# The halves of the weight chunks at moving places, and loads five chunks ahead, in a two-layer decoder

## The chip, the cores and the metric

The kernel runs on one core of one Trainium2 chip. The metric is the device time of one execution, in microseconds (us), taken as the median of several runs. The engines are named as in the profile: PE (TensorE matmuls), PEld (its weight loads), DVE (VectorE), ACT (ScalarE), POOL (GpSimd) and SP (SyncE, which here issues nearly all DMAs; SPq is its queue).

## The reference: a decoder trunk of two layers

All is float32: 256 tokens, width 2048, feed-forward width 5632.

- Layer 0: h += gMLP(rmsnorm(h)): z = gelu(x W_in), split into u and v; v is normed and mixed over tokens by a causal 128 x 128 matrix per group; (u * mixed) W_out. Then h += convFFN(rmsnorm(h)): x W_up, a causal convolution of width 3 per channel, silu(gate) * value, W_down.
- Between the layers, shared keys, values and forget gates: rmsnorm(h) W_kvf, keys normed per head.
- Layer 1: forgetting attention (16 heads of 128, with its own queries and output gate), then the same kind of convFFN with its own weights.
- A last rmsnorm.

The weights are some 418 MB, each used once, for 256 tokens.

## The kernel before

**Float32 by two halves.** Every operand of the large products is the sum of two fp32r values: hi (a rounded copy) and lo (the rest). A product a*b is computed as hi*hi + hi*lo + lo*hi. Activations are kept as one tile with both parts beside each other, `[128, K/128, 512]`: columns 0 to 255 hi, 256 to 511 lo, for one 128-row of features each. Such tiles are X1 (the normed residual, in the profile X), `mlp_X2`, `att_X2` and H (`ffn0_H`, `ffn1_H`; in the profile ffn_H).

**The weight stream.** The weights come in 786 chunks of 128 x 1024 float32 (512 KB; two half chunks at the very start, and one smaller for the forget gates). The class `Stream` holds them in one list, in the order of use. For each chunk there are three steps:

- `_load` (L62 to L71): SP issues the DMA into a `raw` tile. The tile has `LOADS - AHEAD + 1` buffers, which is 4.
- `_split` (L73 to L84): ACT copies raw into `whi` (L82), DVE writes raw - hi into `wlo` (L83). Both tiles have `AHEAD + 1`, 4, buffers of 4096 bytes a partition.
- `mult`: the matmuls of the chunk.

`run` (L86 to L102) goes through the list: in step i it issues the load of chunk i + 6 (`LOADS`), the split of chunk i + 3 (`AHEAD`), and the matmuls of chunk i. After them `advance` moves every pending generator one step: these are the epilogues (evictions, convolution, norms, attention heads), so their instructions come between the chunks in each engine's order. The order of each engine is the order of the program; a buffer is written again when its last readers are done. So the load of a chunk waits in SP's queue for the DVE half of the split of the chunk that had its raw buffer.

**Two kinds of chunk.** All matmuls are recorded at one helper line (L165).

- A feature chunk (`feat_block`, L167): 4 rows of 128 features by 256 outputs. The weights are stationary, 128 x 128 at a time, and the activations move. hi takes eight matmuls of 512 columns (both parts of the activation), lo takes eight of 256 columns (the hi part alone). A pair of outputs (m = 0, 1) alternates between two PSUM banks. In the last chunk of a block lo comes first. There are 656 such chunks: 416 move X1 (W_in's u half, both W_up, the output gate), 176 move H (both W_down), 32 move `mlp_X2` and 32 `att_X2`.
- A token chunk (`tok_block`, L190): 2 rows of 128 features by 512 outputs. The activations are stationary, and the weights move, 512 columns at a time: for each of two token halves hi by hi, lo by hi, hi by lo. There are 129, two of them halves, for W_in's v half, the queries, the keys and the values.

**Where things lie.** Tiles lie in SBUF in the order in which they are made in a pool, each rounded up to 32 bytes: col, h, X1, acc, rB, rcol, ident, ones; then the stream's pool (4 raw, 4 whi, 4 wlo); then small tiles (warm, sq, rsqrt's scratch, half); then the pool of the phase (mlp, ffn0, att, ffn1), which begins with X2 or H.

**The start.** The input x comes in eight slices (`load_input`), each loaded in front of a chunk of the first token block, and prepared (`input_prep`, into X1) in front of that chunk's split. Two tiles for the token mixing of 1 MB each (`load_mix`, L348) are loaded by SP in front of the first chunk of the third token block.

Of the kernel before, what the change touches and what calls it, by code (L numbers as in the profile page):

```python
# [11 lines left out]
F32R = mybir.dt.float32r  # L12
# [5 lines left out]
P = 128  # L18
# [4 lines left out]
KF = FFN // P  # L23
NH = 16
CHUNK = 1024
EPS = 1e-6
SCALE = 128 ** -0.5
AHEAD = 3
LOADS = 6
NEG = -3e38  # L30


# [7 lines left out]
class Stream:  # L40
# [21 lines left out]
    def _load(self, i):  # L62
# [3 lines left out]
        if src is None:  # L66
            return
        raw = self.pool.tile([P, CHUNK], F32, name="raw", tag="raw", bufs=LOADS - AHEAD + 1)
        raw = raw[:, :src.shape[1]]
# [3 lines left out]
    def _split(self, i):  # L73
        if self.items[i][3]:
            self.items[i][3]()
        raw = self.raw.pop(i, None)
        if raw is None:
            return
        n = raw.shape[1]
        hi = self.pool.tile([P, CHUNK], F32R, name="whi", tag="whi")  # L80
        lo = self.pool.tile([P, CHUNK], F32R, name="wlo", tag="wlo")
        self.nc.scalar.activation(hi[:, :n], raw, AF.Copy)  # L82
        self.nc.vector.tensor_tensor(lo[:, :n], raw, hi[:, :n].bitcast(F32), op=OP.subtract)  # L83
        self.parts[i] = (hi, lo)  # L84

    def run(self):  # L86
        n = len(self.items)
        for i in range(-LOADS, n):
            if 0 <= i + LOADS < n:
                self._load(i + LOADS)  # L90
            if 0 <= i + AHEAD < n:
# [41 lines left out]
def build(ctx, tc, d, out):  # L133
# [94 lines left out]
    def rsqrt(y, v, n):  # L228

        t = small.tile([P, n], F32, name="rs_t", tag=f"rs_t{n}", bufs=2)  # L230
        nc.vector.tensor_scalar(y.bitcast(I32), v.bitcast(I32), -0.5, 1597463007.0, op0=OP.mult, op1=OP.add)
        for _ in range(3):
            nc.vector.scalar_tensor_tensor(t, y, -0.5, y, op0=OP.mult, op1=OP.mult)
            nc.vector.tensor_tensor(t, t, v, op=OP.mult)
            nc.vector.scalar_tensor_tensor(y, t, 1.5, y, op0=OP.add, op1=OP.mult)

    def token_sums(rest=None):
# [7 lines left out]
        v = small.tile([P, 2], F32, name="ts_v", tag="ts_v", bufs=2)  # L245
        nc.vector.tensor_scalar(v, mp[:, :2], 1.0 / D, EPS, op0=OP.mult, op1=OP.add)
        rsqrt(rcol, v, 2)
# [108 lines left out]
    def v_done(blk):  # L356
        def done(ps):
# [8 lines left out]
            if blk == 3:  # L366
                v = small.tile([P, 2], F32, name="ts_v", tag="ts_v", bufs=2)
                rv = ph.keep("rv", [P, 2])
                nc.vector.tensor_reduce(v, ss, axis=AX.X, op=OP.add)
                nc.vector.tensor_scalar(v, v, 1.0 / D, EPS, op0=OP.mult, op1=OP.add)  # L370
                rsqrt(rv, v, 2)
# [78 lines left out]
    def head_norm(key, blk, gain):  # L450

        def done(ps):
            dst = att(key)
            for tb in range(2):
# [5 lines left out]
                nc.vector.tensor_reduce(v, sq.rearrange("p (a b) -> p a b", a=4), axis=AX.X, op=OP.add)  # L460
                nc.vector.tensor_scalar(v, v, 1.0 / P, EPS, op0=OP.mult, op1=OP.add)
                rsqrt(r, v, 4)
# [192 lines left out]
def feat_chunks(w, order=None):  # L655
# [5 lines left out]
    a = a.reshape(K // 512, 4, P, N // 256, 256)  # L661
    return np.ascontiguousarray(a.transpose(3, 0, 2, 1, 4)).reshape(-1, P, CHUNK)


def tok_chunks(w):

    K, N = w.shape
    a = w.reshape(K // 256, 2, P, N // 512, 512)
    return np.ascontiguousarray(a.transpose(3, 0, 2, 1, 4)).reshape(-1, P, CHUNK)

# [42 lines left out]
```

## Time and profile before

| | |
|---|---|
| median of 3 runs | 2261.58 us (2261.07 to 2261.91) |
| the profiled execution: its time, its span | 2261.96 us, 2260.2 us |
| mean granted TensorE clock | 0.997 |
| PE busy | 2239.9 us, 99%, 12440 matmuls |
| PEld busy | 1930.5 us, 85% |
| DVE busy | 1529.2 us, 68% |
| ACT busy | 1191.5 us, 53% |
| read from HBM | 417.88 MB, mean 186 GB/s over the span |

The span runs from the first to the last instruction of one execution. Busy times add up the instructions of an engine; those of PE overlap one another, so a busy PE says that matmuls are under way, not how fast they follow one another. How fast is read from the starts of instructions in order of time, or from the number of matmuls in a window.

### The profile page before, as it was taken

The page shows a single profiled execution, that of the slowest core. Times are in us where ns is not written, and L with a number is a line of the kernel's source. Part 1 is how long each engine was busy: PE and PEld are TensorE (multiplying, and loading weights), DVE is VectorE, ACT ScalarE, POOL GpSimd, SP SyncE. Part 2 cuts the span into 40 slices and gives each one's busy share as a digit, 9 for nine tenths or more (in the row PEclk, how much of TensorE's full clock was granted, in tenths as well). Part 3 has the DMA queues.
Part 4 walks back from the last instruction along what each step waited for, and adds up shares of the span by engine and source line. Part 5 has one row for each costly group of instructions (what it writes and reads, how often), then busy time and mean ns, then how long its engine had stood idle before and what let it go on. Part 6 is the DMA issues. An engine that isn't in the chain of part 4 may idle for free.

```text
span 2260.2 us, 32221 instructions
## 1 busy us (share of the span) xinstructions
PE 2239.9 (99%) x12440; PEld 1930.5 (85%) x12440; DVE 1529.2 (68%) x2212; ACT 1191.5 (53%) x1622; POOL 34.6 (2%) x56
## 2 busy tenths in 40 slices
PE   8999999999999999999999999999999999999997
PEld 6888888888888888888788888888888888888886
DVE  6576677777777755457786567677777777764554
ACT  6544455555555544345444666446555555553442
POOL 3000000000000000000000110000000000000000
PEclk9999999999999999999999999999999999999998
DMA  7555555555555555555565555555556555556553
GB/s 280 187 191 170 187 192 190 192 190 193 188 187 187 196 186 176 201 187 171 170 189 183 164 164 187 178 194 187 190 193 190 193 188 194 187 179 202 188 186 113
DMA packets 116442, 422.11 MB, mean 187 GB/s; under 512 B 13232, under 2 KB 13376, under 8 KB 116032
## 3 DMA queue, kind: packets, MB, share of 16 engines
q1 hardware_dynamic: 115344, 417.93, 56.2%
q0 software_dynamic: 768, 2.10, 0.4%
q8 instruction: 97, 1.59, 0.3%
q14 instruction: 57, 0.47, 0.1%
q10 hardware_dynamic: 176, 0.02, 0.0%
HBM read 417.88 MB, written 2.11 MB: 186 GB/s over the span
## 4 chain that ended last, share of the span: by engine, by line
PE 98%; DVE 1%; ACT 0%; DMA 0%; issue 0%; SPq 0%; DVEq 0%
PE ps L165 96%; PE mp L387 0%; PE mp L471 0%; PE mp L557 0%; PE mp L572 0%; DMA h<-xT 0%; DVE wlo L83 0%; DVE X L221 0%; PE mp L580 0%; PE mp L581 0%; PE mp L556 0%; PE mp L579 0%; DVE h L313 0%; PE mp L243 0%; ACT X L220 0%
## 5 line engine op out<-in xcount | busy, mean ns | idle before, releaser
L83 DVE TENSOR_TENSOR wlo<-raw,whi 128x1024 fp32r<-128x1024 f32 (+1 forms) x786 | 953.6, 1222 | 391.2 <-ACT whi L82 383.6
L82 ACT ACTIVATE whi<-raw 128x1024 fp32r<-128x1024 f32 (+1 forms) x786 | 822.5, 1053 | 390.4 <-PE ps L165 355.6
L165 PE MATMUL ps<-X,whi 128*128 128x512 f32 x3328 | 829.6, 396 | 0.0
L165 PEld LDWEIGHTS ps<-X,whi 128*128 128x128 f32 x3328 | 602.3, 188 | 120.7
L165 PEld LDWEIGHTS ps<-X,wlo 128*128 128x128 f32 x3328 | 425.9, 188 | 28.3
L165 PE MATMUL ps<-X,wlo 128*128 128x256 f32 x3328 | 430.6, 277 | 0.0
L165 PE MATMUL ps<-ffn_H,whi 128*128 128x512 f32 x1408 | 354.2, 395 | 0.0
L165 PEld LDWEIGHTS ps<-ffn_H,whi 128*128 128x128 f32 x1408 | 253.5, 188 | 48.3
L165 PEld LDWEIGHTS ps<-ffn_H,wlo 128*128 128x128 f32 x1408 | 190.4, 188 | 14.6
L275 ACT ACTIVATE half<-ps 128x512 f32<-128x512 f32 x104 | 62.1, 597 | 256.0 <-PE ps L165 256.0
L165 PE MATMUL ps<-ffn_H,wlo 128*128 128x256 f32 x1408 | 193.3, 281 | 0.0
L276 DVE TENSOR_TENSOR ffn_a<-ps,half 128x512 f32<-128x512 f32 x88 | 60.9, 692 | 175.3 <-ACT half L275 175.3
L165 PE MATMUL ps<-whi,X 128*128 128x512 f32 x512 | 163.6, 397 | 6.3 <-ACT whi L82 6.3
L165 PE MATMUL ps<-whi,att_X 128*128 128x512 f32 x512 | 169.3, 402 | 0.0
L421 DVE SCALAR_TENSOR_TENSOR ffn_c<-ffn_a,col,ffn_c 128x255 f32<-128x255 f32 x352 | 161.7, 480 | 6.3
L417 ACT ACTIVATE ffn_c<-ffn_a,col 128x256 f32<-128x256 f32 x176 | 96.4, 595 | 47.1 <-DVE ffn_a L277 47.1
L165 PEld LDWEIGHTS ps<-whi,X 128*128 128x128 f32 x512 | 97.1, 190 | 27.2 <-ACT whi L82 6.3
L165 PEld LDWEIGHTS ps<-whi,att_X 128*128 128x128 f32 x512 | 96.1, 188 | 22.2
L165 PE MATMUL ps<-wlo,X 128*128 128x512 f32 x256 | 101.0, 395 | 1.1 <-DVE wlo L83 1.1
L165 PE MATMUL ps<-wlo,att_X 128*128 128x512 f32 x256 | 101.0, 395 | 0.0
L220 ACT ACTIVATE X<-h,col 128x256 fp32r<-128x256 f32 x64 | 29.0, 501 | 104.1 <-DVE h L284 101.5
L225 ACT ACTIVATE ffn_H<-ffn_c 128x256 fp32r<-128x256 f32 x88 | 36.9, 419 | 69.5 <-DVE ffn_c L425 69.5
(140 smaller groups left out, 1228.8 us busy)
## 6 DMA issues: line engine op xcount, KB each, us to landing
raw<-up SPq DMA_DIRECT2D x352, 512.0 KB, 3.7
raw<-down SPq DMA_DIRECT2D x176, 512.0 KB, 4.2
raw<-a_in_u SPq DMA_DIRECT2D x32, 512.0 KB, 3.6
raw<-a_out SPq DMA_DIRECT2D x32, 512.0 KB, 4.1
raw<-b_q SPq DMA_DIRECT2D x32, 512.0 KB, 4.3
raw<-kvf_k SPq DMA_DIRECT2D x32, 512.0 KB, 4.0
raw<-kvf_v SPq DMA_DIRECT2D x32, 512.0 KB, 3.7
raw<-b_g SPq DMA_DIRECT2D x32, 512.0 KB, 3.3
```

The source lines that it names most:

```text
L82: self.nc.scalar.activation(hi[:, :n], raw, AF.Copy)
L83: self.nc.vector.tensor_tensor(lo[:, :n], raw, hi[:, :n].bitcast(F32), op=OP.subtract)
L165: nc.tensor.matmul(o, a, b, start=start, stop=stop, skip_group_check=True)
L220: nc.scalar.activation(dst[:, kt, :T], h[:, kt, :], AF.Copy, scale=g)
L225: nc.scalar.activation(dst[..., :T], src, AF.Copy)
L275: nc.scalar.activation(t, ps[:, :, T:], AF.Copy)
L276: nc.vector.tensor_tensor(a, ps[:, :, :T], t, op=OP.add)
L417: nc.scalar.activation(c[:, m, :], a[:, m, :], AF.Identity, scale=w[2], bias=column(C_CONVB + l * 2 * KF + f))
L421: nc.vector.scalar_tensor_tensor(c[:, m, n:], a[:, m, :T - n], w[k], c[:, m, n:], op0=OP.mult, op1=OP.add)
```

## The change

Each `whi` and `wlo` buffer becomes 128 elements (512 bytes) longer. The part that is used, still 1024 elements, begins at an offset that goes with the number i of the list item: 16 x (i mod 32) bytes for hi, 16 x (7i mod 32) for lo. Since 7 and 32 have no common factor, both go through 32 places in 32 chunks, in different orders. `LOADS` goes from 6 to 5, by which `raw` has three buffers in place of four, and the load of chunk i + 5 is issued in step i. Splits stay three chunks ahead.

```diff
 CHUNK = 1024
+PAD = 128
 ...
 AHEAD = 3
-LOADS = 6
+LOADS = 5
 ...
         n = raw.shape[1]
-        hi = self.pool.tile([P, CHUNK], F32R, name="whi", tag="whi")
-        lo = self.pool.tile([P, CHUNK], F32R, name="wlo", tag="wlo")
+        hi = self.pool.tile([P, CHUNK + PAD], F32R, name="whi", tag="whi")
+        lo = self.pool.tile([P, CHUNK + PAD], F32R, name="wlo", tag="wlo")
+        hi = hi[:, 4 * (i % 32):][:, :CHUNK]
+        lo = lo[:, 4 * (7 * i % 32):][:, :CHUNK]
         self.nc.scalar.activation(hi[:, :n], raw, AF.Copy)
```

In bytes per partition: raw 4 x 4096 becomes 3 x 4096, whi and wlo 8 x 4096 become 8 x 4608; the sum is the same.

## The prediction

> **What bounds the kernel now.** I read the page first: span, engine shares, the chain that ended last.
>
> ```profile
> span 2260.2 us, 32221 instructions
> PE 2239.9 (99%) x12440; PEld 1930.5 (85%) x12440; DVE 1529.2 (68%) x2212; ACT 1191.5 (53%) x1622; POOL 34.6 (2%) x56
> ```
>
> ```profile
> PE 98%; DVE 1%; ACT 0%; DMA 0%; issue 0%; SPq 0%; DVEq 0%
> ```
>
> TensorE (PE) holds 98% of the chain, so I asked next what it waits for, and what the queue that loads the weights waits for. Columns of the waits: total us, times, longest.
>
> ```profile
> PE ps L165 <- DVE wlo L83: 1.1, 3, 0.4
> ```
>
> ```profile
> SPq L70 <- DVE wlo L83: 1534.0, 587, 8.9
> ```
>
> Once started, the matmuls of the weight stream wait 1.1 us in all for their weights. A saturated PE can still be slow, so the third view is the windows, which give matmuls per 100 us (the count behind PE), and the fourth the order of time, where the start of a run of matmuls less the start of the run before gives the real interval (the mean ns of one overlaps its neighbours).
>
> ```profile
> 600.00:700.00 100.00, 100.00 (x579) 87.06 (x578) 76.11 (x110) 59.18 (x83) 0.00 (x0) 1.00 0.59 190
> 800.00:900.00 100.00, 100.00 (x570) 87.21 (x568) 52.42 (x54) 40.06 (x45) 0.00 (x0) 1.00 0.56 187
> ```
>
> ```profile
> 599.41 2.02 PE L165 MATMUL ps<-X,whi 128*128 128x512 f32 x8
> 601.27 1.07 PE L165 MATMUL ps<-X,wlo 128*128 128x256 f32 x8
> 602.19 2.02 PE L165 MATMUL ps<-X,whi 128*128 128x512 f32 x8
> ```
>
> ```profile
> 806.92 1.11 PE L165 MATMUL ps<-ffn_H,wlo 128*128 128x256 f32 x8
> 807.87 2.02 PE L165 MATMUL ps<-ffn_H,whi 128*128 128x512 f32 x8
> 809.74 1.11 PE L165 MATMUL ps<-ffn_H,wlo 128*128 128x256 f32 x8
> ```
>
> Both windows have the clock at 1.00 and PE at 100%, yet X gives 579 matmuls and ffn_H 570 for the same mix of sizes. The runs say where: the eight 512-column matmuls with hi take 1.86 us on X (599.41 to 601.27) and 1.87 on ffn_H; the eight 256-column ones with lo take 0.92 us on X (601.27 to 602.19) but 0.95 on ffn_H (806.92 to 807.87), 119 ns each against 115. A chunk is 2.78 us on X (599.41 to 602.19; 16 x 100/579 = 2.76) and 2.82 on ffn_H (806.92 to 809.74; 16 x 100/570 = 2.81).
>
> These are the same instructions on the same weight buffers, and what differs is where the moving tile lies. By the sizes of the tiles in the order in which they are made, each rounded up to 32 bytes, whi and wlo lie 64 bytes past X1 within 512 (rcol and ones are the only odd sizes between), and 288 past H (224 bytes of small tiles follow wlo). The three tiles that are H, the mlp X2 and the att X2 begin at one address. So the trace already holds two of the 32 relative places: **64, at 2.77 us a chunk, and 288, at 2.81** (means of the two readings).
>
> **The change part by part.** *Instructions:* none is added or removed; splits stay at 786 and matmuls at 12440. The split's operands move by multiples of 16 bytes, its lengths don't:
>
> ```profile
> L83 DVE TENSOR_TENSOR wlo<-raw,whi 128x1024 fp32r<-128x1024 f32 (+1 forms) x786 | 953.6, 1222 | 391.2 <-ACT whi L82 383.6
> L82 ACT ACTIVATE whi<-raw 128x1024 fp32r<-128x1024 f32 (+1 forms) x786 | 822.5, 1053 | 390.4 <-PE ps L165 355.6
> ```
>
> I cost the shifted split at nothing. The cover is PE's lead: whi waited for PE for 355.6 us, so the split stands ready before it is wanted. Were each split a tenth longer, 0.12 us x 786 = 96 us would fall on a DVE that is 68% busy, behind PE. Only a split so long that DVE fills up would show.
>
> *Addresses:* one raw buffer less frees 4 KB, and 8 x 512 bytes take 4 KB, so every other tile stays where it is, and every buffer of hi and lo still begins at the same place within 512. Place p of hi is p = i mod 32, of lo 7i mod 32. Both kinds of chunk then walk through all 32 relative places (X from 64, ffn_H from 288), so both should come to the same mean, if the relative place is what counts.
>
> *What the mean of the places is* is the price that decides. Rows for the counts:
>
> ```profile
> L165 PE MATMUL ps<-X,whi 128*128 128x512 f32 x3328 | 829.6, 396 | 0.0
> L165 PE MATMUL ps<-ffn_H,whi 128*128 128x512 f32 x1408 | 354.2, 395 | 0.0
> ...
> L165 PE MATMUL ps<-mlp_X,whi 128*128 128x512 f32 x256 | 63.8, 396 | 0.0
> L165 PE MATMUL ps<-att_X,whi 128*128 128x512 f32 x256 | 63.7, 395 | 0.0
> ```
>
> That is 3328/8 = 416 chunks on X and (1408 + 256 + 256)/8 = 240 on the other address. Of the 32 places I know two, 2.77 and 2.81; their mean is 2.79. X loses 0.02 us x 416 = 8.3 us and the others gain 0.02 x 240 = 4.8: **+3.5 us**. The bounds: if the mean is as good as X's place, 240 x -0.04 = -9.6; if it is as bad as ffn_H's, 416 x 0.04 = +16.6. A third sample is the forget chunk, where the weights are only 16 columns and walk by 64 bytes per pair against one moving address:
>
> ```profile
> 1113.01 0.40 PE L165 MATMUL ps<-att_X,whi 128*16 128x512 f32 x1
> ...
> 1117.86 0.40 PE L165 MATMUL ps<-att_X,whi 128*16 128x512 f32 x1
> ```
>
> Fourteen pairs in 4.85 us are 0.346 a pair, 2.77 for eight: X's value, by loads an eighth as long. It pulls towards the lower bound, but those loads have less to collide with, so I stay with the middle. All places seen so far are multiples of 32 bytes; half of the new ones aren't, and no row prices those.
>
> The token chunks stream the weights and hold X. Their rows, one hi pair per three matmuls:
>
> ```profile
> 59.85 0.62 PE L165 MATMUL ps<-whi,X 128*128 128x512 f32 x2
> ...
> 69.47 0.62 PE L165 MATMUL ps<-whi,X 128*128 128x512 f32 x2
> ...
> 1137.86 0.40 PE L165 MATMUL ps<-wlo,att_X 128*128 128x512 f32 x1
> 1138.56 0.39 PE L165 MATMUL ps<-wlo,att_X 128*128 128x512 f32 x1
> ```
>
> 14 threes in 9.62 us are 229 ns a matmul on X, and 0.70 us a three are 233 on att_X. With 768 matmuls each, a mean of 231 costs 1.5 us on the one and gives 1.5 on the other: **0**, bounds -3 and +3.
>
> *Loads five ahead.* A load waits until the split of the chunk that had its buffer is done (the 1534 us of SP's waits above): now the chunk four before it, then three, so each load goes out about one chunk later. All that SP issues in this order moves with it (the input slices, the second part of col, the two mixing tiles). A steady case:
>
> ```profile
> 606.59 0.33 SPq L70 DMA_DIRECT2D raw<-up  x1
> 609.89 1.22 DVE L83 TENSOR_TENSOR wlo<-raw,whi 128x1024 fp32r<-128x1024 f32 x1
> 615.34 1.06 ACT L82 ACTIVATE whi<-raw 128x1024 fp32r<-128x1024 f32 x1 [0.48 <-PE ps L165]
> ```
>
> ```profile
> DMA to landing us min/median/max: 2.8/3.9/9.7
> ```
>
> The load at 606.59 is split at 615.34. Afterwards it goes out at 611.1 (609.89 + 1.22) and lands at 615.0 by the median: still before ACT wants it. It may be some tenths late by a slower landing, and PE has three split chunks, 8.3 us, in hand. Price 0 there; without that lead half a microsecond per block of four chunks would be about 100 us. Two places have less in hand. They are the start and the loading of the mixing tiles:
>
> ```profile
> 27.04 1.06 ACT L82 ACTIVATE whi<-raw 128x1024 fp32r<-128x1024 f32 x1 [2.24 <-DMA raw<-a_in_v]
> ...
> 39.49 0.42 SPq L351 DMA_DIRECT2D mlp_bB<-bs  x1
> ...
> 50.43 1.06 ACT L82 ACTIVATE whi<-raw 128x1024 fp32r<-128x1024 f32 x1 [4.88 <-DMA raw<-a_in_v]
> ...
> 55.48 0.69 ACT L361 ACTIVATE mlp_vt<-ps,rcol 128x512 f32<-128x512 f32 x1 [2.70 <-PE ps L165]
> ```
>
> At the start ACT already waits 2.24 us for a chunk, at 27.04, and PE hardly sees it: its waits there, the 1.1 us above, are for DVE's lo. Loads one chunk later, 2.8 us, prolong such waits of ACT. Behind the mixing tiles the split at 50.43 opens the next block, which PE begins when it ends the one evicted at 55.48. 2.8 us later it ends at 54.3, and its lo at 55.5: just in time. Both places together 0 to 4 us; I take **+0.5**, near the end that the rows favour.
>
> *Sum:* 3.5 + 0 + 0.5 = +4.0 us. The profiled execution took 2261.96 us, 1.76 more than its span, and lies 0.4 above the median of 2261.58; the change in the span carries over: 2261.6 + 4.0 = **2265.6**.
>
> **The rivals.** *The place does nothing (no effect beyond the loads).* The intervals could differ by the moving tile's own place, 32 bytes past a multiple of 64 for X and at one for H, and not by the distance to the weights. Then shifting the weights moves nothing, and the time is 2261.6 to 2262.6. For it: hi takes the same 1.86 and 1.87 us at both distances. Against it: the token chunks, whose moving tile is the weights, also differ, 229 to 233. The Trainium skill is on this rival's side: "TensorE: Matmul & The Clock Gate", in its step-by-step part, says that moving rows and weight loads have two independent read ports, so that loading the next weights takes nothing from the running matmul; by that rule the answer would be 2261.6. The trace does not settle it.
>
> *The mean place is like ffn_H's (slower).* X's lo at 115 ns is the shortest interval of a 256-column matmul in these rows. If X sits at one of few free places, 416 chunks lose it: +16.6 us, nothing for the others, 2278.7; with places worse than both, 2.84 say, 0.07 x 416 + 0.03 x 240 = +36, 2298. It decides from a mean of 2.792 on: 656 chunks x (2.792 - 2.785, the weighted mean now) is 4.5 us. For it: the 115; against it: the forget chunk at 2.77.
>
> *A fixed distance is the disease (faster).* 512 columns take 229 ns in the token chunks on X, and 233 everywhere else. If most places give 229 and 115, a chunk is 8 x 344 = 2.75: -0.02 x 416 - 0.06 x 240 = -23 us, 2239; half of that is 2250. Against it: hi is alike at both known distances.
>
> **How the numbers follow.** A measurement of this kernel tells about 0.2%, 4.5 us, from no change. The forecast (mean between the two places) has 0.42, its own range 2252 to 2274; no place effect 0.13; like ffn_H or worse 0.22; faster 0.23. The forecast lies close to the edge: of its 0.42, 0.20 is slower, 0.19 within, 0.03 faster. With 0.01 of the rival without effect: slower 0.43, same 0.31, faster 0.26. The range reaches half into both outer rivals, to 2240 and 2284, leaving out some 0.12 below and 0.08 above.
>
> **What would show it.** Right: the 100-us windows on X fall from 579 to about 575 matmuls and those on ffn_H rise from 570 to about 575; chunk lengths repeat every 32 chunks; the intervals of lo on X spread from 115 upwards. Wrong: windows unchanged (no place effect), both below 570 (bad places), both above 579 (cured). The loads are right if matmuls of the weight stream wait for whi or wlo no more than 1 us beyond now; ACT waiting for raw a few us more is expected and costs nothing. Any wait of PE for wlo in the windows after 100 us makes the load step wrong.

## The result, and the profile after

The changed kernel takes **2275.52 us** (median of 4; 2273.80 to 2275.98), the kernel before 2261.74 (median of 4) measured beside it. The ratio is **1.0060, interval 1.0047 to 1.0073**: 13.8 us, or 0.6%, slower. That is three times the 0.2% that can be told from no change. It lies inside the predicted range, 1.5 us outside the forecast's own range, and 9.9 us above the predicted time.

The page of the changed kernel, its span and engines, then its chain that ended last:

```profile
span 2273.9 us, 32221 instructions
PE 2250.8 (99%) x12440; PEld 1942.4 (85%) x12440; DVE 1530.0 (67%) x2212; ACT 1191.9 (52%) x1622; POOL 35.0 (2%) x56
...
PE 97%; DVE 2%; DMA 1%; ACT 0%; issue 0%; POOL 0%; SPq 0%; DVEq 0%; ACTq 0%; POOLq 0%
```

The instructions are the same in number, 32221, and PE still holds nearly the whole chain. The span grew by 13.7 us (2260.2 to 2273.9) and PE's busy time by 10.9, so most of the loss lies where PE is at work. (Three lines were added: L165 of before is L168 here, L82 and L83 are L85 and L86, L471 is L474.)

Groups by line and form, busy us, mean ns of one, idle us. The two rows of before that the prediction did not show:

```profile
L165 PE MATMUL ps<-X,wlo 128*128 128x256 f32 x3328 | 430.6, 277 | 0.0
...
L165 PE MATMUL ps<-ffn_H,wlo 128*128 128x256 f32 x1408 | 193.3, 281 | 0.0
```

and the four groups of the changed kernel:

```profile
L168 PE MATMUL ps<-X,whi 128*128 128x512 f32 x3328 | 827.1, 395 | 0.0
L168 PE MATMUL ps<-X,wlo 128*128 128x256 f32 x3328 | 444.8, 281 | 0.0
L168 PE MATMUL ps<-ffn_H,whi 128*128 128x512 f32 x1408 | 352.8, 394 | 0.0
L168 PE MATMUL ps<-ffn_H,wlo 128*128 128x256 f32 x1408 | 192.1, 280 | 0.0
```

One group lost: lo on X, 430.6 to 444.8, **+14.2 us**. The other three gained: hi on X 829.6 to 827.1 (-2.5), hi on ffn_H 354.2 to 352.8 (-1.4), lo on ffn_H 193.3 to 192.1 (-1.2).

The windows of the changed kernel (number of matmuls is the count behind PE):

```profile
400.00:500.00 100.00, 100.00 (x574) 87.38 (x573) 76.03 (x108) 58.99 (x81) 0.00 (x0) 1.00 0.58 187
600.00:700.00 100.00, 100.00 (x570) 87.17 (x569) 75.36 (x108) 58.69 (x81) 0.00 (x0) 1.00 0.57 187
800.00:900.00 100.00, 100.00 (x575) 87.54 (x574) 52.12 (x53) 41.55 (x45) 0.00 (x0) 1.00 0.58 188
```

On X 579 has become 570 to 574, on ffn_H 570 has become 575, with the clock at 1.00 and PE at 100% in all of them. In order of time:

```profile
640.13 1.08 PE L168 MATMUL ps<-X,wlo 128*128 128x256 f32 x8
641.05 2.02 PE L168 MATMUL ps<-X,whi 128*128 128x512 f32 x8
642.90 2.04 PE L168 MATMUL ps<-X,wlo 128*128 128x256 f32 x16
644.78 1.57 PE L168 MATMUL ps<-X,whi 128*128 128x512 f32 x6
```

The first eight lo take 0.92 us (640.13 to 641.05), 115 ns each; the next sixteen, of two other chunks, 1.88 (642.90 to 644.78), 117.5 each. So lo now differs from chunk to chunk. To see how, I took, for every matmul of the feature chunks, the time from its start to the start of the next matmul, sorted by the place of the half against the moving tile. Places are bytes, and only their remainder by 256 is kept, since places 256 apart came out alike (within about 1 ns; an experiment below tries it at one place). Mean ns, 208 matmuls each:

| place past X1 | 0 | 16 | 32 | 48 | 64 | 80 | 96 | 112 |
|---|---|---|---|---|---|---|---|---|
| lo, 256 columns | 118.3 | 118.6 | 117.8 | 119.8 | **115.6** | 119.2 | 117.8 | 119.6 |
| hi, 512 columns | 233.1 | 231.3 | 233.9 | 233.0 | 235.8 | 232.1 | 234.8 | 233.4 |

| place past X1 | 128 | 144 | 160 | 176 | 192 | 208 | 224 | 240 |
|---|---|---|---|---|---|---|---|---|
| lo, 256 columns | 119.5 | 120.1 | 119.5 | 118.3 | 116.4 | 116.8 | 117.3 | 118.4 |
| hi, 512 columns | 234.2 | 232.6 | 234.1 | 230.7 | 233.3 | 231.9 | 233.4 | 229.4 |

Of sixteen places the one that the kernel before held on X all the time, 64, is the best for lo, and the worst for hi. The table has to be read with care: both offsets go by the same i, so each place of lo always meets the same place of hi (lo at 64 meets hi at 64, lo at 16 meets hi at 240), and what it prices are sixteen pairs, each also behind the same chunk. Means over all: lo on X 114.0 before and 118.3 now, hi on X 233.7 and 232.9; on the other address (H and the two X2, where the place was 32) lo 118.8 and 118.0, hi 232.8 and 231.9. The lengths of neighbouring X chunks repeat every 16 chunks (over the 176 chunks of the first W_up the correlation is 0.87 at a distance of 16 chunks, and -0.05 at 15).

As sums: X, 3328 x (118.3 - 114.0) = +14.3 and 3328 x (232.9 - 233.7) = -2.4 us; the other address, 1936 matmuls of either kind, -1.5 and -1.7. Together **+8.7 us by places**. The remaining 5.0 of the span's 13.7 lie in token chunks and in epilogues between them. PE's waits in the changed kernel that bear on it (total us, times, longest):

```profile
PE mp L474 <- DVE att_big L468: 2.5, 2, 2.4
PE mp L246 <- POOL acc L273: 1.5, 1, 1.5
```

Neither of them is a wait for weights, and neither is among PE's waits in the kernel before. The experiments take the two parts in turn.

### The profile page after: what moved, and what is told of

Read it like the earlier page. It is cut to its first block, busy times and chain, and to the rows that moved or that the text cites. A ratio compares the mean times of both kernels' runs of the same rounds, so it can differ in the third digit from the quotient of the medians.

```text
span 2273.9 us, 32221 instructions
## 1 busy us (share of the span) xinstructions
PE 2250.8 (99%) x12440; PEld 1942.4 (85%) x12440; DVE 1530.0 (67%) x2212; ACT 1191.9 (52%) x1622; POOL 35.0 (2%) x56
## 4 chain that ended last, share of the span: by engine, by line
PE 97%; DVE 2%; DMA 1%; ACT 0%; issue 0%; POOL 0%; SPq 0%; DVEq 0%; ACTq 0%; POOLq 0%
PE ps L168 95%; DVE wlo L86 0%; PE mp L390 0%; PE mp L474 0%; PE mp L560 0%; DMA raw<-a_in_v 0%; DMA h<-xT 0%; PE mp L575 0%; DMA raw<-kvf_k 0%; ACT whi L85 0%; PE mp L583 0%; PE mp L584 0%; PE mp L559 0%; PE mp L582 0%; DVE h L316 0%
## 5 line engine op out<-in xcount | busy, mean ns | idle before, releaser
L86 DVE TENSOR_TENSOR wlo<-raw,whi 128x1024 fp32r<-128x1024 f32 (+1 forms) x786 | 953.4, 1221 | 413.3 <-ACT whi L85 405.2
L85 ACT ACTIVATE whi<-raw 128x1024 fp32r<-128x1024 f32 (+1 forms) x786 | 822.5, 1053 | 420.1 <-PE ps L168 302.4
L168 PE MATMUL ps<-X,whi 128*128 128x512 f32 x3328 | 827.1, 395 | 0.0
L168 PEld LDWEIGHTS ps<-X,whi 128*128 128x128 f32 x3328 | 603.7, 188 | 119.8
L168 PEld LDWEIGHTS ps<-X,wlo 128*128 128x128 f32 x3328 | 437.0, 188 | 27.4
L168 PE MATMUL ps<-X,wlo 128*128 128x256 f32 x3328 | 444.8, 281 | 0.0
L168 PE MATMUL ps<-ffn_H,whi 128*128 128x512 f32 x1408 | 352.8, 394 | 0.0
L168 PEld LDWEIGHTS ps<-ffn_H,whi 128*128 128x128 f32 x1408 | 253.4, 188 | 48.0
L168 PEld LDWEIGHTS ps<-ffn_H,wlo 128*128 128x128 f32 x1408 | 188.5, 188 | 14.0
L168 PE MATMUL ps<-ffn_H,wlo 128*128 128x256 f32 x1408 | 192.1, 280 | 0.0
L168 PE MATMUL ps<-whi,X 128*128 128x512 f32 x512 | 164.2, 398 | 6.2 <-ACT whi L85 6.2
L168 PE MATMUL ps<-whi,att_X 128*128 128x512 f32 x512 | 169.7, 403 | 0.0
L168 PEld LDWEIGHTS ps<-whi,X 128*128 128x128 f32 x512 | 97.0, 189 | 28.1 <-ACT whi L85 6.2
L168 PEld LDWEIGHTS ps<-whi,att_X 128*128 128x128 f32 x512 | 96.9, 189 | 21.7
L168 PE MATMUL ps<-wlo,X 128*128 128x512 f32 x256 | 102.2, 399 | 0.0
L168 PE MATMUL ps<-wlo,att_X 128*128 128x512 f32 x256 | 101.3, 396 | 0.0
```

The lines of the kernel that those rows point to most:

```text
L168: nc.tensor.matmul(o, a, b, start=start, stop=stop, skip_group_check=True)
```

## The experiments

Except where said, the diff is against the kernel before, and the ratio is to the kernel before beside it. Interval means are worked out as above, from all starts of a kind.

**The loads alone.**

```diff
-LOADS = 6
+LOADS = 5
```

> The kernel before with LOADS = 5 alone; the weights keep their places. Theory (most of the 13.8 us is the places, the loads cost little): +1 to +4 us against before, from a later start (0.8 us by 50 us in the profile after) and from a wait of PE for the head norms among the key chunks (2.5 us in the profile after); the 256-column matmuls on X stay at 114 ns. Rival (the fifth load ahead is the main cost): +8 to +14 us, with these intervals still at 114 ns and waits of PE in many places.

Measured: 2266.51 us against 2261.44, ratio 1.0024 (1.0014 to 1.0034), **+5.1 us**, a little above the expected 1 to 4. All matmuls of feature chunks keep their intervals (lo on X 114.0). The two waits of PE found above are here too, and the timeline of this kernel shows how the larger comes about:

```profile
1225.78 1.06 ACT L82 ACTIVATE whi<-raw 128x1024 fp32r<-128x1024 f32 x1 [4.26 <-DMA raw<-kvf_v]
1226.74 0.67 ACT L457 ACTIVATE sq<-ps,rcol 128x512 f32<-128x512 f32 x1
...
1231.17 0.69 DVE L465 TENSOR_TENSOR att_big<-ps,att_hr 128x512 f32<-128x512 f32 x1
...
1232.01 0.63 PE L471 MATMUL mp<-ident,att_big 128*128 128x128 f32 x4 [2.82 <-DVE att_big L465]
...
1232.78 0.63 PE L165 MATMUL ps<-wlo,att_X 128*128 128x512 f32 x1
...
1233.21 1.05 PE L165 MATMUL ps<-whi,att_X 128*128 128x512 f32 x2
```

The same place in the kernel before:

```profile
1218.87 1.05 ACT L82 ACTIVATE whi<-raw 128x1024 fp32r<-128x1024 f32 x1
...
1219.82 0.68 ACT L457 ACTIVATE sq<-ps,rcol 128x512 f32<-128x512 f32 x1
...
1222.37 1.06 ACT L82 ACTIVATE whi<-raw 128x1024 fp32r<-128x1024 f32 x1 [1.87 <-DMA raw<-kvf_v]
```

ACT works in program order: a split, the square of a head's norm (L457), the next split. Before, the split ahead of the square found its chunk landed, and the wait for a load, 1.87 us, fell on the split behind it. With one raw buffer less it falls on the split ahead of the square and is 4.26 us. Nothing on PE wants that split yet. But the square is late with it, then the chain on DVE that makes the norm (4.4 us from the square to L465, 1226.74 to 1231.17), and then the transposes at L471, which stand in PE's order ahead of the next weight matmuls: PE waits 2.82 us, with weights ready. Then comes a second price. The windows (the clock stands behind POOL's count):

```profile
1228.00:1232.00 4.00, 1.19 (x6) 0.64 (x5) 3.55 (x16) 1.36 (x2) 0.00 (x0) 1.00 0.41 131
1232.00:1236.00 4.00, 3.99 (x13) 3.21 (x14) 3.35 (x3) 1.63 (x2) 0.00 (x0) 0.58 0.46 141
```

Behind the gap the granted clock is 0.58, and a 512-column matmul takes 0.43 us (1232.78 to 1233.21) in place of 0.23. Some eight such matmuls, 1.6 us, and the wait make about 4.4 us. The same happens in small near 28 us, where ACT waits for raw, the squares of the first norm are late, and POOL's sum of them holds PE for 1.5 us (in the changed kernel the second of the two waits above). In this execution the clock falls there too:

```profile
32.00:36.00 4.00, 4.00 (x15) 3.15 (x14) 1.94 (x6) 0.83 (x2) 0.00 (x0) 0.68 0.55 176
```

The second price is not paid each time. The changed kernel has the same wait of 1.5 us near 28 us with the clock at 1.00 behind it, and behind its wait of 2.4 us the clock is 0.67 (1236 to 1240 us). The kernel with alternating places, below, waits 2.3 us for the same transposes and keeps 1.00. That may be why the nine runs of this kernel spread over 4 us (2264.48 to 2268.62), where the kernel before spreads over 1; the profiled one, with two such stretches, took 2268.26.

**Five ahead, but with the fourth raw buffer kept.**

```diff
-LOADS = 6
+LOADS = 5
-        raw = self.pool.tile([P, CHUNK], F32, name="raw", tag="raw", bufs=LOADS - AHEAD + 1)
+        raw = self.pool.tile([P, CHUNK], F32, name="raw", tag="raw", bufs=LOADS - AHEAD + 2)
```

> The kernel with LOADS = 5 but four raw buffers, places as before. Theory (the 5 us of the loads come from the buffer that is missing, not from the order in which SP issues): SP issues the same loads in the same order and waits for the same splits as before: no change, 2261 to 2262, no wait of PE for the head norms. Rival (the later issue is what costs): 2265 to 2268.

Measured: 2261.46 against 2261.73, ratio 1.0000 (0.9991 to 1.0009). The 5.1 us are gone: they come from the missing buffer, and the step in which a load stands in the program costs nothing. That the walk with four raw buffers would take 5 us less follows by addition and was not tried.

**X's place alone, from 64 to 160.** A gap of 96 bytes behind `ones` moves the stream's tiles and everything after them away from X1; the distance to H stays.

```diff
+    gap = const.tile([P, 24], F32, name="gap")
```

> The kernel before with a gap of 96 bytes between ones and the stream's tiles: all weights lie 160 bytes past X1 within 256 in place of 64, while their distance to H and to X2 stays. Theory (the distance between the moving tile and the weights sets the interval): the lo matmuls on X go from 114 to about 120 ns, the hi ones stay at 233, those on H don't change; 5.8 ns x 3328 = +19 us, 2278 to 2284. Rival (the place of the moving tile alone counts, X1 not having moved): no change, 2261 to 2263.

Measured: 2286.99 against 2261.44, ratio 1.0113 (1.0099 to 1.0127), **+25.6 us**. The group and the window on X:

```profile
L166 PE MATMUL ps<-X,wlo 128*128 128x256 f32 x3328 | 450.4, 282 | 0.0
```

```profile
600.00:700.00 100.00, 100.00 (x568) 87.04 (x567) 74.30 (x105) 57.31 (x80) 0.00 (x0) 1.00 0.58 187
```

lo on X goes from 114.0 to 120.0 ns: 3328 x 6.05 = 20.1 us. hi adds 1.6 and the token chunks on X 3.9, which I had not counted: that is the miss by 3 us over the expected range. Nothing of the program changed but 96 bytes of free space, so a placement alone moves this kernel by more than 1%.

**Everything moved by 96 bytes, distances kept.** The same gap, now behind col and so ahead of h, X1 and all that follows.

```diff
+    gap = const.tile([P, 24], F32, name="gap")
```

> The kernel before with the same gap of 96 bytes ahead of h: X1, the weights, H and X2 all move by 96 bytes, every distance between them stays. Theory (distance): no change, within 2 us of before, lo on X 114 ns and on H 119. Rival (own place of the moving tile, 32 bytes past a multiple of 64 being good): X1 comes to a multiple of 64 and H to 32 past one, so lo on X goes to 119 and on H to 114: 5 x 3328 - 5 x 1920 ns = +7 us.

Measured: 2261.70, ratio 1.0001 (0.9992 to 1.0010); the group is to the tenth that of the kernel before:

```profile
L166 PE MATMUL ps<-X,wlo 128*128 128x256 f32 x3328 | 430.6, 277 | 0.0
```

So it is the distance between moving tile and weights that counts, and not where either lies.

**X's place moved by 256 bytes, to 320.** The gap of the 160 experiment, with 64 elements.

> The kernel before with a gap of 256 bytes between ones and the stream's tiles: the weights lie 320 bytes past X1 in place of 64, the distance to H stays. Theory (distance, with a period of 256 bytes, as the intervals of the kernel after repeat): no change, lo on X 114 ns. Rival (period 512): place 320 is another place, lo on X at some 116 to 118 ns, +6 to +13 us.

Measured: 2261.49 against 2261.73, ratio 1.0000 (0.9990 to 1.0009), with lo on X at 114.0 again. At this place another 256 bytes change nothing, and the table's places 256 apart came out alike: the distance counts only within **256 bytes**. Of the 32 places of the change sixteen are copies, which is why the chunk lengths repeat after 16.

**H's place alone, to 192.** 96 bytes behind wlo, in front of the phase's pool.

```diff
-    warm = small.tile([P, 2], F32, name="warm")
+    warm = small.tile([P, 2 + 24], F32, name="warm")[:, :2]
```

> The kernel before with a gap of 96 bytes behind the stream's tiles: X1 and the weights stay, H and X2 move by 96, so that the weights lie 192 bytes past them in place of 288 (32 past 256). Theory (distance, as the kernel after shows it for this place: lo 113.5 to 118 ns, hi 229 to 233): lo on H from 119 to 114 to 118 and hi from 233 to 229 to 233, 1920 of each: -3 to -17 us, the middle -8. Rival (own place): H at 32 past a multiple of 64 gives lo 114 and leaves hi: -9.6 us; it is the run with everything moved that tells these two apart. No change here would refute both.

Measured: 2249.49 against 2261.44, ratio 0.9947 (0.9935 to 0.9960), **-12.0 us**. Its groups on ffn_H:

```profile
L165 PE MATMUL ps<-ffn_H,whi 128*128 128x512 f32 x1408 | 348.9, 392 | 0.0
...
L165 PE MATMUL ps<-ffn_H,wlo 128*128 128x256 f32 x1408 | 189.5, 278 | 0.0
```

hi 354.2 to 348.9, lo 193.3 to 189.5, and likewise for the two X2; in intervals 232.8 to 229.2 and 118.8 to 116.1. X is as before. The place that the table of the walk calls good is good when it is held.

**Both halves at 192, on X and H.** 128 bytes ahead of the stream's pool, 96 behind it.

```diff
+    gap = const.tile([P, 32], F32, name="gap")
...
+    warm = small.tile([P, 2 + 24], F32, name="warm")[:, :2]
```

> The kernel before with gaps of 128 bytes ahead of raw and 96 behind wlo: hi and lo both lie 192 bytes past X1, H and X2. Theory (distance): H as in the run that moved it alone (hi 229, lo 116), X the same: hi -3.6, lo +2 ns, 3328 of each: 5 us better than that run, 2244. Rival (H and X behave differently at one distance): X keeps hi at 233, and lo goes to 116 or more: 2256 or slower.

Measured: 2246.64 against 2261.73, ratio 0.9934 (0.9920 to 0.9947), -15.1 us. On X hi falls from 233.7 to 230.0 (-12.1 us), lo rises from 114.0 to 115.8 (+6.0), and the token chunks on X rise by 4. These 4 us were not in the expected 2244, which it misses by 2.6.

**hi at 192, lo at 64, on X and H.** 128 bytes ahead of the stream's pool, 128 between whi and wlo, 224 behind. The idea was to give each half its own best place.

```diff
+        if i == 0:
+            self.pool.tile([P, 32], F32, name="gap2", tag="gap2", bufs=1)
...
+    gap = const.tile([P, 32], F32, name="gap")
...
+    warm = small.tile([P, 2 + 56], F32, name="warm")[:, :2]
```

> The kernel before with three gaps (128 bytes ahead of raw, 128 between whi and wlo, 224 behind wlo), so that hi lies 192 and lo 64 bytes, within 256, past X1 and past H and X2 alike. Theory (distance, and each half's own interval goes by its own place): hi on X from 233 to 229 ns, hi on H the same, lo on X stays at 114, lo on H from 119 to 114 to 118; 3.6 x 5248 + 3 x 1920 ns = about -25 us, 2231 to 2242. Rival (the two halves disturb each other, so that a good place holds only while both lie at the same): less than the 12 us gained by moving H alone, or a loss.

Measured: 2247.14 against 2261.73, ratio 0.9936 (0.9923 to 0.9950), -14.6 us where at least 20 were expected. The group shows why:

```profile
L168 PE MATMUL ps<-X,wlo 128*128 128x256 f32 x3328 | 436.9, 279 | 0.0
```

lo on X did not move, it lies at 64 as before, yet it went from 430.6 to 436.9: 116.0 ns in place of 114.0. So a half's cost hangs on the other half's place too. How, the trace doesn't say: in the four chunks of a block the eights of lo take 117.8, 117.6, 114.7 and 113.8 ns (in the kernel before 113.8 to 114.1 in all four), although the first three of them alike follow a run of hi.

**Does a change of place from chunk to chunk cost by itself?** Three raw buffers as in the change, buffers of 64 elements more, both halves alternating by 128 bytes with the chunk's number: places 64 and 192 on X.

```diff
-LOADS = 6
+LOADS = 5
...
+        hi = hi[:, 32 * (i % 2):][:, :CHUNK]
+        lo = lo[:, 32 * (i % 2):][:, :CHUNK]
```

> LOADS = 5, and hi and lo both alternate from chunk to chunk between two places 128 bytes apart (within 256: 64 and 192 past X1, 32 and 160 past H and X2); buffers of 4352 bytes. The reference point is the kernel with LOADS = 5 alone, 2266.5. On X both places are known as constant ones: 8 x (232.8 + 114.0) and 8 x (229.3 + 115.8) ns a chunk. Theory A (the interval depends on the place alone): X at the mean, 7 ns a chunk less than at 64, x 416 = -3 us, H within 1 us: 2262 to 2265. Theory B (the matmuls carry a phase over from the chunk before, so a place that changes costs more than a constant one; in the kernel after, X with both halves at 192 takes 351 ns a pair, but 345 where the place is constant): lo on X above 115.5 ns on average and a chunk on X 15 to 30 ns longer than at 64, +6 to +12 us: 2271 to 2279.

Measured: 2269.10 against 2261.46, ratio 1.0034 (1.0022 to 1.0047); 2.6 us above the loads alone, which met neither theory's figure. hi on X follows the place (234.0 at 64, 229.8 at 192, as when held). lo does not: 115.3 at 64 and 117.3 at 192, against 114.0 and 115.8 when held. That is 1.4 ns on 3328 matmuls, 4.7 us, which the places alone don't explain. It looks like a carry-over from one chunk to the next, or from one half to the other, at these two places.

**The walk, slower.** To tell whether that carry-over makes the mean of the walk, every place is held for eight chunks. The diff is against the changed kernel.

```diff
-        hi = hi[:, 4 * (i % 32):][:, :CHUNK]
-        lo = lo[:, 4 * (7 * i % 32):][:, :CHUNK]
+        hi = hi[:, 4 * (i // 8 % 32):][:, :CHUNK]
+        lo = lo[:, 4 * (7 * (i // 8) % 32):][:, :CHUNK]
```

> The kernel after, but with i // 8 in place of i in both offsets: the same 32 pairs of places, each kept for eight chunks and then left, in place of one chunk. The feature chunks meet each pair about equally often in both kernels. Theory A (a place has its price, whatever came before): the same mean, 2273 to 2278. Theory B (a chunk that begins at another place than the one before begins in a worse phase): most chunks now follow one at their own place, so lo on X comes below the 118.3 ns of the kernel after, by 1 to 3 ns, and the time to 2264 to 2273.

Measured: 2274.04 against 2261.73, ratio 1.0058 (1.0043 to 1.0072), so the time of the change.

```profile
L168 PE MATMUL ps<-X,whi 128*128 128x512 f32 x3328 | 826.8, 395 | 0.0
L168 PE MATMUL ps<-X,wlo 128*128 128x256 f32 x3328 | 444.7, 281 | 0.0
```

444.7 us of lo on X beside 444.8: the mean is that of the places, and the step from place to place adds nothing to it. At single places it does count (lo at 64 is 114.0 here, as when held, and 115.6 in the change), others pay it back. By pairs, one interval of hi plus one of lo on X, this run gives 345.5 ns with both at 192, 347.0 with both at 64, 349.3 or more for the other fourteen, and 351.0 as the mean. So the pair that the kernel before holds on X is the second best of the sixteen when it is held.

**A version that beats both.** Back to six ahead. X's feature chunks have hi at 192 (an offset of 32 elements for those chunks alone), so that the token chunks keep hi at 64; lo at 192 on X; on H and the X2 hi at 192 and lo at 64. The other two blocks on X1 get the 32 as well, `chunk` keeps it in `self.place`, and `big` in the attention phase gets 5 buffers in place of 6, for the room.

```diff
+        hi = self.pool.tile([P, CHUNK + 64], F32R, name="whi", tag="whi")
+        hi = hi[:, self.place[i]:][:, :CHUNK]
+        if i == 0:
+            self.pool.tile([P, 32], F32, name="gap", tag="gap", bufs=1)
...
-    def feat_block(src, x, K, done):
+    def feat_block(src, x, K, done, place=0):
...
+            feat_block(d[f"up{l}"][4 * i:4 * i + 4], lambda: X1, KD, up_done(l, i), 32)
...
+    warm = small.tile([P, 2 + 56], F32, name="warm")[:, :2]
```

> Six loads ahead as before; hi at 192 and lo at 192 for feature chunks on X, hi at 192 and lo at 64 for those on H and X2, hi at 64 for token chunks on X1 (by gaps, and by buffers of hi that are 256 bytes longer with an offset of 128 for the feature chunks on X). The room comes from att_big, five buffers in place of six. If the places act as in the runs before: X -6 us (run with both at 192), H and X2 -13 us (run with 192 and 64), token chunks -1 to +1: 2240 to 2244. Rival (five buffers of att_big hold up the heads): waits of PE among the heads, 2245 to 2250.

Measured: **2242.76 us** against 2261.46, ratio **0.9917 (0.9902 to 0.9932)**, -18.7 us, as expected. Groups and windows:

```profile
L169 PE MATMUL ps<-X,whi 128*128 128x512 f32 x3328 | 817.8, 393 | 0.0
L169 PE MATMUL ps<-X,wlo 128*128 128x256 f32 x3328 | 437.2, 279 | 0.0
...
L169 PE MATMUL ps<-ffn_H,wlo 128*128 128x256 f32 x1408 | 187.5, 278 | 0.0
```

```profile
400.00:500.00 100.00, 100.00 (x583) 88.11 (x582) 76.67 (x111) 59.68 (x83) 0.00 (x0) 1.00 0.59 192
800.00:900.00 100.00, 100.00 (x580) 87.85 (x579) 55.42 (x59) 43.18 (x49) 0.00 (x0) 1.00 0.55 185
```

583 and 580 matmuls in 100 us, against 578 or 579 and 570 before. hi on X pays 829.6 - 817.8 = 11.8 us, lo takes 6.6 back, H gives the rest.

**The same with hi on X at 240**, the cheapest place for hi in the table (an offset of 44 elements in place of 32).

> As the run with places by kind, but hi at 240 for the feature chunks on X. In the kernel after, hi on X took 230.1 ns at 240 against 233.1 at 192, and 229.3 at a constant 192. If 240 is as good at rest as it is in the walk, or better, X gains 0 to 2 ns a hi matmul over the run with places by kind, 0 to -7 us; rival: lo, at 192, enters its slow state more often behind it, 0 to +7 us.

Measured: 2246.45 against 2261.46, ratio 0.9934 (0.9920 to 0.9948): 3.7 us behind the version with 192.

```profile
L169 PE MATMUL ps<-X,whi 128*128 128x512 f32 x3328 | 814.7, 392 | 0.0
L169 PE MATMUL ps<-X,wlo 128*128 128x256 f32 x3328 | 443.6, 280 | 0.0
```

hi gains 3.1 more (817.8 to 814.7), but lo, whose own place is still 192, loses 6.4 (437.2 to 443.6). As with 192 and 64, a half pays for where the other lies; in the table hi at 240 had met lo at 16.

## Why the prediction was right or wrong

The sign was the likeliest one in the chances, and the mechanism named (the place of the weights against the moving tile, plus loads that come late) is what the experiments show. The sum was +4.0 us and the measurement +13.8: 8.7 by places, by the starts of the changed kernel, and 5.1 by loads, by the run with that edit alone. That these add up to the tenth is luck, as the runs with that edit spread over 4 us; that 5.0 us of the span lie outside the feature chunks is read from the changed kernel itself. Two terms were mis-sized.

**The instructions, 0: right.** The split's groups in the changed kernel:

```profile
L86 DVE TENSOR_TENSOR wlo<-raw,whi 128x1024 fp32r<-128x1024 f32 (+1 forms) x786 | 953.4, 1221 | 413.3 <-ACT whi L85 405.2
L85 ACT ACTIVATE whi<-raw 128x1024 fp32r<-128x1024 f32 (+1 forms) x786 | 822.5, 1053 | 420.1 <-PE ps L168 302.4
```

1221 and 1053 ns a piece, beside 1222 and 1053: offsets by multiples of 16 bytes cost ACT and DVE nothing.

**The places, +3.5 forecast, +8.7 measured: mis-sized.** The step that failed is "their mean is 2.79". A chunk by mean intervals is 8 x (114.0 + 233.7) = 2.782 us on X before, and after 8 x (118.3 + 232.9) = 2.810; on the other address 2.813 became 2.799. X came to the value that I had put down as the upper bound of the mean, 2.81, and H to the middle: two addresses that walk through the same places ended 0.01 us apart, so "both should come to the same mean" held only roughly. The two halves depend on each other, and the two addresses don't meet the same pairs (hi at 240 comes with lo at 16 on X and with lo at 208 on H). The error was to take two known places as a fair sample of all. One of them, X's, was the best of sixteen for lo, as the table shows, and as a pair, held, the second best of sixteen, as the slower walk shows; and the rival "the mean place is like ffn_H's" said just that from the 115 ns. By its price (+16.6, nothing for the others) it overstated: X lost 11.9 and the others gained 3.2. The truth lay between forecast and rival. The forget chunk, which spoke for the lower bound, misled.

Half of the new places are odd multiples of 16 bytes, which no row priced. On X they are 1.1 ns worse than the even ones for lo (118.9 and 117.8, means of the table) and 2.3 ns better for hi (231.8 and 234.1): as a group they are not what made the walk slow.

**Token chunks, 0 within 3: right for this change.** Against the kernel before, the query chunks of the changed kernel take 0.9 us more in all, and those of keys and values, away from the wait at the transposes, no more than before. But the term isn't idle: a constant bad place cost them 3.9 us on X in the experiment with 160.

**Loads, +0.5 (bounds 0 to 4) forecast, +5.1 measured: wrong, and outside its bounds.** The step looked for one thing, PE waiting for whi or wlo, and put "any wait of PE for wlo after 100 us" as the sign against itself. No such wait came. The forecast that ACT would wait longer for raw and that this "costs nothing" is what failed: ACT's queue holds the epilogues too, and a square behind a late split held DVE's chain, and through the transposes PE. I priced the step that moved by who reads its result, and not by what stands behind it on its engine. The two places the prediction named were the start, where some of it did fall, and the mixing tiles, where it didn't; the largest wait, in the chunks of the values, was not looked at, although its 1.87 us stood in the trace of before.

**What would show it.** The windows on ffn_H rose to 575 as said; on X they fell to 570 to 574, a little below the "about 575". lo on X does spread upwards from 115, to 120. Chunk lengths repeat, though after 16 chunks and not 32.

**The rival "the place does nothing"** is refuted by 96 bytes of free space: +25.6 us when they stand between X1 and the weights, 0 when they stand ahead of both. With it goes, for this kernel, what I had drawn from the rule set beside it. The Trainium skill ("TensorE: Matmul & The Clock Gate", the step-by-step part) gives moving rows and weight loads two independent read ports. By that rule, as I used it, no distance between the two should matter, and the kernels in which only places differ should all have taken 2261.6. The measurement decides: the interval of the same matmul goes from 114.0 to 120.0 ns with the distance alone. Whether it is a read port, or something else that the distance governs, no run here shows.

**The rival "a fixed distance is the disease"** had it the wrong way round for the walk: most places are no better than 32 or 64, and a mean over all is worse than a good one held. What it saw in the rows, 229 ns for 512 columns against 233, is real: hi at 192 on H takes 229.2. Places chosen and held gave 18.7 of the 23 us that it promised.

**Open** stays why the distance counts, why the cost of lo depends on the place of hi, and what makes lo at 192 cost 115.8 behind hi at 192 and 117.9 behind hi at 240. The price of a pair of places was found by measuring it, and no rule for pairs came out.

## What to carry to other kernels

When the same matmul has different start-to-start intervals against different tiles, look at the distance of the tiles within 256 bytes early; a gap of some bytes in a pool tries it, and a walk through all places only buys the mean, which here was worse than what the kernel already held. Price a load that comes later by everything that stands behind its first reader on that engine, epilogues included, and follow these to the busiest engine. And when few samples carry a mean, ask whether one of them is the best there is.

## What the runs showed of the hardware that was not expected

- The interval of a matmul on the weight stream depends on the distance between moving tile and stationary weights, within 256 bytes: 114.0 to 120.0 ns for 256 columns and 229.1 to 234.1 for 512, with places held. Moving both by 96 bytes changes nothing, moving one by 256 nothing, moving one by 96 up to 25.6 us in 2261.
- The two halves are not independent: lo at place 64 takes 114.0 ns beside hi at 64 and 116.0 beside hi at 192.
- A stall of 2.82 us on PE was followed by a granted clock of 0.58 over the next 4 us, and by matmuls of 0.43 us in place of 0.23. The Trainium skill ("TensorE: Matmul & The Clock Gate", Part 1 on the clock gate) states half clock after an idle window of about 3.4 us, and 426.7 ns for 512 columns at half clock. The second agrees with the 0.43; the stall here was shorter than the window that the page names, and the clock fell all the same, in this execution behind a wait of 1.5 us too. The length of the wait alone doesn't decide it: behind 2.4 us in the changed kernel the clock fell (0.67), behind 2.3 us in the one with alternating places it stayed at 1.00.
